# Four token tiles abreast in the first head, inverse rms by DRAM rows, and new shares in an encoder layer

## The chip, the cores and the metric

The kernel runs on one core of a Trainium2 chip. The metric is the device time of one execution in microseconds (us). TensorE (PE in the profile) multiplies, with the load of its stationary operand shown as PEld; VectorE (DVE), ScalarE (ACT) and GpSimd (POOL) do the elementwise work, and one queue, that of SyncE (SP), issues every DMA.

## The reference

One layer of a bidirectional encoder is applied to two requests of 1024 tokens and 1024 channels, in float32. Each request goes through the same steps:

```python
h = rms_norm(x, norm_g) * (1.0 + scale) + shift          # shift, scale, gate from silu(c) @ w_ada
qa, ka, va, za, qb, kb, vb, zb, ga, gb = split(h @ w_in)  # 5376 columns
oa = gqa_attention(rope(rms(qa)), rope(rms(ka)), va) * silu(za)     # 8 heads of 64, 2 kv heads
ob = rms_norm(diff_attention(rope(rms(qb)), rope(rms(kb)), vb, lam)) * silu(zb)  # 4 heads, 2 maps each
merged = sigmoid(ga) * (oa @ w_proj_a) + sigmoid(gb) * (ob @ w_proj_b)
y = x + gate * (merged @ w_out)
```

## The kernel before

Every factor of a projection is split into a high part that the multiplier takes exactly and a low part, the rest; a product is the sum of three matmuls (high by high, high by low, low by high). `load_w` loads a block of 256 columns of a weight in four pieces (two chunks of 128 channels each) and `split_w` makes the high part on ACT (L195) and the low part on POOL or, for every other piece while `alone[0]` is set, on DVE (L197).

**Start.** `start` loads the modulation weights in eight tiles; `ada` multiplies each (L330), `ada_end` copies the accumulator of each pair (L348) and lays it out as columns (L342). The first half of the first request's tokens is normalised and modulated there, chunk by chunk of 128 channels (chunks 4 to 7 later than 0 to 3, as their modulation comes last). The second half follows in `start_late`: its sums of squares (L297), an inverse root on POOL (L307), four transposes that spread it over all partitions (L314), one copy of that (L316), eight scalings on DVE (L418), and then per chunk two ACT operations and the low part on DVE (L423).

**Head.** `head` makes the keys and values of branch A with `kva_gen`: eight token tiles of 128, one after another, each of 24 matmuls 128x256 (`proj_tt`, L574) into a PSUM bank `f`. Behind each tile stands a chain: `rms` (ACT copies and squares, DVE sums, POOL takes the root, L597), the rope (L600 to L626), and, two tiles later, a transpose (L637) with the copies of `pairs_T`. With `alone[0]` set the rope is DVE's. Woven in are the gate products `z_gen` (24 matmuls 128x512, L764) and then the first queries.

**Order.** `weave` draws from several generators by shares and leads (the tables at the top of the file): attention steps, projections, gate pieces. From the order so recorded a scheduler makes each engine's own order, with priorities and with pairs that `behind` ties. In attention, scores go into one of two PSUM banks `s` (L798, L799), DVE takes the maximum and ACT the exponential (L802), DVE flips the probabilities (L843), DMAs place them as tile `q`, and PE multiplies them by the values (L866 and L883).

**End of a request.** `gated_gen` multiplies the attention outputs by their inverse sums. For branch A these go through DRAM: one transpose, a row, a store to `rA`, and broadcast loads. For branch B (`e` of 4 to 7) four transposes per half head (L970) spread the inverse rms into a PSUM bank, from which DVE scales (L971). `merge_gen` then projects branch A in 16 pieces of 12 matmuls and branch B in 16 more (L1038); the last `TAIL` pieces of branch A come after attention has ended.

## Time and profile before

| | |
|---|---|
| runs of the kernel | 1879.2, 1880.7 and 1883.36 us, median 1880.7 |
| span of the profiled execution | 1880.0 us |
| busy PE, DVE, ACT, POOL | 1836.5, 1222.3, 780.1, 607.1 us |
| mean granted clock of PE | 0.995 |
| DMA | 295.46 MB, mean 157 GB/s |

The span runs from the first to the last instruction of one profiled execution; the runs are of other executions. A busy PE is not PE at its peak, as matmuls are pipelined and their ends are modelled; so the distance from one start to the next is used below as the time of a matmul, not its mean duration.

### The profile page before, as it was taken

The numbers are of one execution on the slowest core, as the hardware profiler recorded it, in microseconds if no ns is written. First come the engines' busy times: TensorE is split into PE (matmuls) and PEld (weight loads), VectorE is DVE, ScalarE is ACT, GpSimd is POOL, SyncE is SP. The second block draws the span as 40 slices with busy tenths as digits, with TensorE's granted clock in tenths as the row PEclk, the third lists the DMA queues.
The fourth block names the chain that finished last, engine by engine and source line by source line (L and its number), as shares of the span: only waits on it lengthen the run. The fifth ranks groups of instructions, "written<-read, shape, count | busy, mean of one in ns | idle before, by whom it ended". The sixth has DMA issues, their size and how long they took to land.

```text
span 1880.0 us, 29891 instructions
## 1 busy us (share of the span) xinstructions
PE 1836.5 (98%) x10398; PEld 1550.6 (82%) x10398; DVE 1222.3 (65%) x2016; ACT 780.1 (41%) x1544; POOL 607.1 (32%) x888
## 2 busy tenths in 40 slices
PE   6999999999999999999999999999999999999999
PEld 3798877888899977888889888888888898888887
DVE  5777766454777777347466687666357766663795
ACT  4544434344554444313223445344345545442241
POOL 1243311433454451221233333014354635222100
PEclk8999999999999999999999999999999999999999
DMA  9135776555444567754631567666524343675442
GB/s 324 57 94 160 208 198 178 146 168 163 111 127 113 162 188 219 244 152 140 206 131 52 156 177 204 189 186 188 158 68 141 106 129 103 176 247 173 128 127 92
DMA packets 283895, 295.46 MB, mean 157 GB/s; under 512 B 41952, under 2 KB 236640, under 8 KB 283744
## 3 DMA queue, kind: packets, MB, share of 16 engines
q1 hardware_dynamic: 283744, 293.54, 53.1%
q8 instruction: 83, 1.36, 0.3%
q14 instruction: 68, 0.56, 0.1%
HBM read 133.98 MB, written 42.01 MB: 94 GB/s over the span
## 4 chain that ended last, share of the span: by engine, by line
PE 68%; DMA 4%; issue 3%; DVE 3%; SPq 3%; POOL 2%; ACT 1%; ACTq 0%; DVEq 0%; POOLq 0%
PE f L764 15%; PE f L574 15%; PE f L1038 7%; PE a L883 5%; PE s L798 4%; PE s L799 4%; PE a L866 4%; PE s L1038 3%; PE f L1073 3%; PE s L1073 2%; PE f L1145 2%; SPq L852 1%; DMA q<-p 1%; DMA st<-in_w_in_dram 1%; PE s L1145 1%
## 5 line engine op out<-in xcount | busy, mean ns | idle before, releaser
L764 PE MATMUL f<-u,w 128*128 128x512 f32 x2232 | 565.1, 395 | 0.8 <-POOL w L197 0.4
L574 PE MATMUL f<-w,u 128*128 128x256 f32 x3456 | 478.6, 287 | 0.9 <-POOL w L197 0.4
L764 PEld LDWEIGHTS f<-u,w 128*128 128x128 f32 x2232 | 409.8, 188 | 82.6 <-POOL w L197 1.1
L574 PEld LDWEIGHTS f<-w,u 128*128 128x128 f32 x3456 | 452.3, 193 | 22.3 <-issue 3.5
L800 DVE TENSOR_REDUCE m<-s 128x1 f32<-128x1024 f32 x256 | 309.6, 1218 | 98.8 <-PE s L799 97.4
L197 POOL TENSOR_TENSOR w<-st,w 128x512 fp32r<-128x512 f32 x160 | 213.2, 1350 | 357.9 <-ACT w L195 342.1
L843 DVE STREAM_TRANSPOSE p<-p 128x1024 f32<-128x1024 f32 x192 | 237.7, 1243 | 87.9 <-ACT p L802 73.5
L802 ACT ACTIVATE p<-s,m,u 128x1024 f32<-128x1024 f32 x128 | 153.9, 1204 | 160.0 <-issue 57.8
L802 ACT ACTIVATE p<-s,m,rsB 128x1024 f32<-128x1024 f32 x128 | 154.0, 1204 | 118.7 <-DVE m L801 97.1
L799 PE MATMUL s<-u,sw 128*128 128x512 f32 x512 | 201.1, 397 | 0.0
L195 ACT ACTIVATE w<-st 128x512 fp32r<-128x512 f32 x184 | 108.2, 626 | 112.4 <-DMA st<-in_w_in_dram 97.5
L1038 PE MATMUL f<-u,w 128*128 128x512 f32 x552 | 131.0, 392 | 0.0
L883 PE MATMUL a<-q,u 128*128 128x256 f32 x512 | 126.5, 380 | 4.0 <-DMA q<-p 3.7
L597 POOL TENSOR_TENSOR rsB<-ss,nhalf 128x4 f32<-128x4 f32 x64 | 68.1, 1064 | 184.7 <-DVE ss L596 160.6
L866 PE MATMUL a<-q,u 128*64 128x256 f32 x1024 | 117.7, 382 | 3.6 <-DMA q<-p 2.9
L1038 PEld LDWEIGHTS f<-u,w 128*128 128x128 f32 x552 | 103.0, 188 | 21.1
L798 PE MATMUL s<-u 128*128 128x512 f32 x256 | 107.9, 425 | 2.7 <-ACT p L802 2.7
L799 PEld LDWEIGHTS s<-u,sw 128*128 128x128 f32 x512 | 96.5, 189 | 16.4
L640 DVE TENSOR_TENSOR u<-f,u 64x256 fp32r<-64x256 f32 (+1 forms) x198 | 81.3, 411 | 42.9 <-ACT u L639 37.5
L883 PEld LDWEIGHTS a<-q,u 128*128 128x128 f32 x512 | 93.5, 190 | 18.8 <-issue 3.4
L772 ACT ACTIVATE ev<-f 128x512 f32<-128x512 f32 x93 | 55.3, 595 | 128.5 <-PE f L764 72.5
L866 PEld LDWEIGHTS a<-q,u 128*64 128x64 f32 x1024 | 73.8, 137 | 40.3 <-issue 7.2
(221 smaller groups left out, 2174.6 us busy)
## 6 DMA issues: line engine op xcount, KB each, us to landing
q<-p SPq DMA_DIRECT2D x768, 128.0 KB, 2.6
st<-in_w_in_dram SPq DMA_DIRECT2D x132, 256.0 KB, 3.3
zd<-ev SPq DMA_DIRECT2D x96, 256.0 KB, 2.7
sw<-u SPq DMA_DIRECT2D x256, 64.0 KB, 2.0
u<-in_w_ada_dram SPq DMA_DIRECT2D x8, 1024.0 KB, 11.7
oo<-zd SPq DMA_DIRECT2D x64, 128.0 KB, 2.4
od<-oo SPq DMA_DIRECT2D x64, 128.0 KB, 2.4
st<-in_w_in_dram SPq DMA_DIRECT2D x64, 128.0 KB, 2.7
```

Source lines behind the costliest of these rows:

```text
L195: hi = nc.scalar.activation(wh, st, AF.Copy)
L197: lo = e.tensor_tensor(out=wl, in0=st, in1=wh.bitcast(F32), op=ALU.subtract)
L574: ins = nc.tensor.matmul(ps, lt[c][:, sl], w[:, c, wi, :], start=(k == 0), stop=(k == 23))
L764: ins = nc.tensor.matmul(ps, w[:, c, wi, e * P : (e + 1) * P], rt[c], start=(k == 0), stop=(k == 23),)
L798: nc.tensor.matmul(s[:, sl], q, k[:, sl], start=True, stop=False)
L799: nc.tensor.matmul(s[:, sl], sw, k[:, sl], start=False, stop=True)
L800: nc.vector.tensor_reduce(out=m, in_=s, axis=AX.X, op=ALU.max, negate=True)
L802: nc.scalar.activation(pt.rearrange("p (j c a) -> p j c a", j=4, c=8), s.rearrange("p (c a j) -> p j c a", c=8, j=4), AF.Exp, bias=m, scal ...
L843: nc.vector.transpose(pt, pt)
L866: lambda k=k, m=m: nc.tensor.matmul(acc[(LO, HI)[m]], u["v"][:, k], pT[m][:, k], start=(k == 0), stop=(k == 7))
L883: nc.tensor.matmul(acc, u["v"][:, k], pT[:, k], start=(k == 0), stop=(k == 7))
L1038: nc.tensor.matmul(ps, w[:, c, wi, d * P : (d + 1) * P], o[:, oi, :], start=(k == 0), stop=(k == 11))
```

## The change

The first head of the first request is written anew. `abreast` puts four token tiles through each chunk of channels before the next chunk (two of their banks are halves of one `s` bank), twice for eight tiles; `kva_first` sets the fronts and transposes around it. The rope of tiles 1, 2, 3, 5 and 7 (`TURNS`) goes to POOL there, and so do two of eight low parts in `start_late`, whose spread now has room of its own in a `p` tile. `LATE` gives the second half's inverse root and scalings a priority. The first five gate blocks (`Z_HEAD`), not three, belong to that head. The last accumulator copy is tied ahead of DVE's weight splits, nine matmuls of the identity (`keep_busy`) follow the last two of the modulation weights, and branch B's small tables are tied behind the head's ropes on DVE.

For branch B the inverse rms of a head is transposed once, copied as a row, stored to a DRAM tile `rB` and loaded as a broadcast into a `tab` tile. All shares and leads of the weave get new values.

```diff
-Z_SHARE = (
-    (5, 16, 3, 1, 0, 17),
-    (6, 14, 2, 0, 3, 18),
-)
-Z_HEAD = (3, 3)
-Z_HEAD_A = (-0.35, -0.25)
-ATT_W = (
-    (1.0, 0.9, 1.1, 0.95, 1.0, 1.52),
-    (1.229, 1.265, 0.9, 1.0, 0.85, 1.069),
-)
-IN_A = (
-    (0.1, 0.05, 0.4, 0.05, -0.05, 0.1),
-    (0.1, 0.05, 0.4, 0.1, 0.15, 0.55),
-)
-Z_A = (
-    (0.15, 0.0, 0.2, -0.1, 0.0, 0.0),
-    (0.2, 0.05, 0.35, 0.05, 0.0, -0.1),
-)
-LAST_ATT, LAST_FILL = (48, 40)
+Z_SHARE = ((4, 15, 3, 1, 0, 20), (6, 14, 2, 0, 3, 18))
+Z_HEAD = (5, 3)
+LATE = (200, 3, 200)
+Z_AT = (2, 3)
+TURNS = (1, 2, 3, 5, 7)
+Z_HEAD_A = (-0.15, -0.05)
+ATT_W = ((1.1, 0.85, 1.1, 0.95, 1.05, 1.62), (1.229, 1.265, 0.8, 1.0, 0.85, 1.569))
+IN_A = ((-0.25, 0.25, 0.4, -0.05, -0.05, 0.15), (0.25, 0.0, 0.55, 0.1, 0.25, 0.7))
+Z_A = ((-0.25, 0.0, 0.2, -0.1, 0.05, 0.0), (0.2, 0.0, 0.35, 0.65, -0.3, -0.05))
+LAST_ATT, LAST_FILL = (47, 37)
 GATED_A = -0.2
-TAIL = 6
-TAIL_A = 0.3
+TAIL = 10
+TAIL_A = 0.05
 LAG = 2
...
-BEHIND = 1.4
-PAIRS = (1.05, 0.3)
+BUSY = (0, 0, 0, 0, 0, 0, 6, 3)
+BEHIND = 1.3
+PAIRS = (1.25, 1.4)
...
             prev = ins
+        return prev
...
-    def split_w(w, q, st):
+    def split_w(w, q, st, after=None):
         wh = w[:, q * 2 : q * 2 + 2, 0, :]
...
         lo = e.tensor_tensor(out=wl, in0=st, in1=wh.bitcast(F32), op=ALU.subtract)
+        if after is not None and e is nc.vector:
+            behind(lo, after)
         if ends and not alone[0]:
...
         for q, st in enumerate(sts):
-            split_w(w, q, st)
+            split_w(w, q, st, copied[0])
+    copied = [None]
...
-    def spread(rs):
+    def spread(rs, room=None):
...
             nc.tensor.transpose(bank[:, k * P : (k + 1) * P], rs[:, k : k + 1].to_broadcast([P, P]), ident)
-        rsb = mtile("ev", [P, 512], bufs=1)
+        rsb = mtile("ev", [P, 512], bufs=1) if room is None else room
         nc.scalar.activation(rsb, bank, AF.Copy)
...
     accs = {}
+    spare = ps_a.tile([P, 512], F32, tag="a", name=nm("a"))
+    def keep_busy(n, other):
+        for _ in range(n):
+            ins = nc.tensor.matmul(spare[:, :P], ident, ident, start=True, stop=True)
+            behind(ins, other)
+            other = ins
...
             accs[n // 2] = gbank()
-        across(accs[n // 2], q, [wt[:, c] for c in range(4)])
+        return across(accs[n // 2], q, [wt[:, c] for c in range(4)])
...
-        together([
+        return together([
             lambda c=c: nc.tensor.matmul(
...
         row = halves2(ptile())[0]
-        nc.vector.tensor_copy(row, acc)
+        copied[0] = nc.vector.tensor_copy(row, acc)
         ps = gbank()[:, :8].rearrange("p (c g) -> p c g", g=2)
...
         for n in range(8):
-            ada(n, wts[n])
+            last = ada(n, wts[n])
+            keep_busy(BUSY[n], last)
             if n == 3:
...
         sq = squares(xT[1])
-        return lambda: start_late(ht, xT, inv_rms(added(sq, end), latest[0]))
+        late_x.extend(xT[1])
+        return lambda: inv_rms(added(sq, end))
-    def start_late(ht, xT, rs):
-        rsb = spread(rs)
+    late_x = []
+    def start_late(ht, rs):
+        rsb = spread(rs, halves2(ptile())[0])
         for c in range(NCH):
-            x = xT[1][c]
+            x = late_x[c]
             if c % 4 == 0:
...
             nc.scalar.activation(ht[1][0][c], x, AF.Copy)
-            nc.vector.tensor_tensor(out=ht[1][1][c], in0=x, in1=ht[1][0][c].bitcast(F32), op=ALU.subtract)
+            e = nc.gpsimd if c % 3 == 2 else nc.vector
+            e.tensor_tensor(out=ht[1][1][c], in0=x, in1=ht[1][0][c].bitcast(F32), op=ALU.subtract)
...
             dma(gB[:, i, :], t[src][0].partition_broadcast(P))
-        nc.vector.tensor_scalar(out=gB[:, 0, :], in0=gB[:, 0, :], scalar1=SC, scalar2=None, op0=ALU.mult)
+        first = nc.vector.tensor_scalar(out=gB[:, 0, :], in0=gB[:, 0, :], scalar1=SC, scalar2=None, op0=ALU.mult)
+        behind(first, chained[1])
         nc.vector.tensor_tensor(out=gB[:, 1, 16:], in0=gB[:, 1, 16:], in1=gB[:, 0, 16:], op=ALU.mult)
...
         lamp = lamw[:, 4 * HD : 6 * HD].rearrange("p (a d) -> p a d", a=2)
-        nc.vector.tensor_tensor(
+        first = nc.vector.tensor_tensor(
             out=lamp, in0=lamv[:, 0::2, :], in1=lamv[:, 1::2, :], op=ALU.mult
         )
+        behind(first, chained[1])
         nc.vector.tensor_reduce(out=lam2, in_=lamp, axis=AX.X, op=ALU.add)
...
         dma(subg, t["subln_g"].rearrange("o e -> e o"))
-        nc.vector.tensor_scalar(out=subg, in0=subg, scalar1=0.5 * (1.0 - LAM_INIT) * math.sqrt(2 * HD), scalar2=None, op0=ALU.mult)
+        first = nc.vector.tensor_scalar(out=subg, in0=subg, scalar1=0.5 * (1.0 - LAM_INIT) * math.sqrt(2 * HD), scalar2=None, op0=ALU.mult)
+        behind(first, chained[1])
...
-    def kva_gen(ht, out):
+    lone = [False]
+    def kva_parts(ht, out):
         w = kva_w.pop()[0] if kva_w else load_w(w_cols(w_in, (C_KA, 256)))
...
         def front(tt, ps):
-            e = by_turns(tt)
+            e = nc.gpsimd if lone[0] and tt in TURNS else by_turns(tt)
             x3, s3 = rms(ps[:, :128], 2, e)
...
+        return w, front, back
+    def kva_gen(ht, out):
+        w, front, back = kva_parts(ht, out)
         yield from pipelined(ht, w, front, back, (0, 0))
+    def abreast(ht, w, hf):
+        both = sbank()
+        banks = [fbank()[:, :256], fbank()[:, :256], both[:, :256], both[:, 512:768]]
+        hh, hl = ht[hf]
+        for c in range(NCH):
+            for i, ps in enumerate(banks):
+                sl = slice(i * P, (i + 1) * P)
+                for n, (lt, wi) in enumerate(((hh, 0), (hh, 1), (hl, 0))):
+                    ins = nc.tensor.matmul(
+                        ps, lt[c][:, sl], w[:, c, wi, :], start=(c == n == 0), stop=(c == 7 and n == 2)
+                    )
+                    if latest[0] is None:
+                        behind(ins, picked[0])
+                    latest[0] = ins
+        return banks
+    def kva_first(ht, out, zs, late):
+        w, front, back = kva_parts(ht, out)
+        lone[0] = True
+        banks = abreast(ht, w, 0)
+        with tc.high_priority(offset=LATE[0]):
+            rs = late()
+        rows = [front(i, banks[i]) for i in range(3)]
+        drain(islice(zs, LATE[1]))
+        with tc.high_priority(offset=LATE[2]):
+            start_late(ht, rs)
+        drain(islice(zs, 6 - LATE[1]))
+        banks = banks + abreast(ht, w, 1)
+        for i in range(8):
+            back(i, rows[i])
+            if i < 5:
+                rows.append(front(i + 3, banks[i + 3]))
+            if i in Z_AT:
+                drain(islice(zs, 3))
+        lone[0] = False
     def qa_gen(st, half):
...
             dma(st["rA"], row)
+        if i > 1 and hf == 0:
+            for h in range(2 * i - 4, 2 * i - 2):
+                ps = fbank()[:NTT, :P]
+                nc.tensor.transpose(ps, st["ssB"][:, h], ident)
+                row = rtile()[:NTT, :P]
+                nc.scalar.activation(row, ps, AF.Copy)
+                dma(st["rB"][h * NTT : (h + 1) * NTT], row)
         rA = st["rA"].rearrange("(j h n) p -> j h (n p)", j=8, h=2)
+        rB = st["rB"].rearrange("(e h n) p -> e h (n p)", e=4, h=2)
         u = utile().rearrange("p (c s n) -> p c s n", c=2, s=2)
...
             dma(o, st["od"][e][hf])
+            rb = mtile("tab", [P, 512])
             if e < 4:
-                rb = mtile("tab", [P, 512])
                 for a in range(2):
...
             else:
-                rb = gbank()
-                for k in range(4):
-                    r = st["ssB"][:, e - 4, hf * 4 + k : hf * 4 + k + 1]
-                    nc.tensor.transpose(rb[:, k * P : (k + 1) * P], r.to_broadcast([P, P]), ident)
+                dma(rb, rB[e - 4, hf].partition_broadcast(P))
             nc.vector.scalar_tensor_tensor(out=o, in0=rb, scalar=subg if e > 3 else 1.0, in1=o, op0=ALU.mult, op1=ALU.mult)
...
         if g == 0:
-            for i in range(2):
-                drain(islice(kva, 6))
-                drain(islice(zs, 3))
-                if i == 0:
-                    late()
-            weave((chain(kva, qa), 40, 0.0), (islice(zs, nz - 6), nz - 6, Z_HEAD_A[g]))
+            kva_first(st["ht"], st, zs, late)
+            weave((qa, 26, 0.0), (islice(zs, nz - 12), nz - 12, Z_HEAD_A[g]))
         else:
...
         st["rA"] = dpool.tile([64, P], F32, name=nm("rA"))
+        st["rB"] = dpool.tile([4 * NTT, P], F32, name=nm("rB"))
         st["od"] = [
```

In each program's own order, DVE works as follows around the last accumulator copy (`p` from `f`) and the two splits of the first weight block (`w`). Before:

```order
L370 TENSOR_TENSOR u_277<-u_166,u_276 128x512 x3
L354 TENSOR_TENSOR modc<-f_301,bcol 128x8
L370 TENSOR_TENSOR u_277<-u_166,u_276 128x512
L197 TENSOR_TENSOR w_184<-p_185,w_184 128x2x256
L348 COPY p_311<-f_294 128x512
L197 TENSOR_TENSOR w_184<-p_188,w_184 128x2x256
L354 TENSOR_TENSOR modc<-s_313,bcol 128x8
L358 TENSOR_TENSOR modc<-modc,gcol 128x8
```

And with the change:

```order
L376 TENSOR_TENSOR u_280<-u_169,u_279 128x512 x4
L360 TENSOR_TENSOR modc<-f_310,bcol 128x8
L354 COPY p_323<-f_297 128x512
L191 TENSOR_TENSOR w_187<-p_188,w_187 128x2x256
L191 TENSOR_TENSOR w_187<-p_191,w_187 128x2x256
L360 TENSOR_TENSOR modc<-s_325,bcol 128x8
L364 TENSOR_TENSOR modc<-modc,gcol 128x8
L372 TENSOR_SCALAR u_170<-u_170,modc 128x512 x2
```

The copy has moved ahead of both splits. PE's order behind it: the layout of that copy (`pick`), and then the first key and value products, two matmuls by the high part of the input and one by its low part per chunk. Before:

```order
L342 MATMUL s_313<-pick,p_311 128x2 x4
L574 MATMUL f_361<-w_184,u_276 128x256 x2
L574 MATMUL f_361<-w_184,u_277 128x256
L574 MATMUL f_361<-w_184,u_276 128x256 x2
L574 MATMUL f_361<-w_184,u_277 128x256
L574 MATMUL f_361<-w_184,u_276 128x256 x2
L574 MATMUL f_361<-w_184,u_277 128x256
L574 MATMUL f_361<-w_184,u_276 128x256 x2
L574 MATMUL f_361<-w_184,u_277 128x256
```

And with the change:

```order
L336 MATMUL f_297<-u_185,cT 32x512 x4
L323 MATMUL a_111<-ident 128x128 x3
L348 MATMUL s_325<-pick,p_323 128x2 x4
L729 MATMUL f_374<-w_187,u_279 128x256 x2
L729 MATMUL f_374<-w_187,u_280 128x256
L729 MATMUL f_375<-w_187,u_279 128x256 x2
L729 MATMUL f_375<-w_187,u_280 128x256
L729 MATMUL s_373<-w_187,u_279 128x256 x2
L729 MATMUL s_373<-w_187,u_280 128x256
L729 MATMUL s_373<-w_187,u_279 128x256 x2
L729 MATMUL s_373<-w_187,u_280 128x256
```

One tile (bank `f_361`) took four chunks in a row; now four tiles (`f_374`, `f_375` and the two halves of `s_373`) take each chunk in turn, and dummies (`a` from the identity) stand ahead of the layout. The other place is PE at the end of the first request's attention, where branch A's projection (`f` or `s` from `u` and `w`) begins. Before:

```order
L970 MATMUL s_8341<-ident,ssB_120 128x128 x4
L1038 MATMUL f_8151<-u_7372,w_8131 128x512 x6
L1038 MATMUL f_8151<-u_7683,w_8131 128x512 x6
L970 MATMUL f_8167<-ident,ssB_120 128x128 x4
L1038 MATMUL f_8177<-u_7372,w_8131 128x512 x6
L1038 MATMUL f_8177<-u_7683,w_8131 128x512 x6
```

And with the change:

```order
L1100 MATMUL f_8250<-u_7512,w_8149 128x512 x6
L1100 MATMUL f_8250<-u_7790,w_8149 128x512 x6
L1015 MATMUL f_8264<-ident,ssB_121 8x128
L1100 MATMUL s_8284<-u_7790,w_8149 128x512 x4
L1100 MATMUL s_8350<-u_7340,w_8314 128x512 x6
L1015 MATMUL f_8269<-ident,ssB_121 8x128
L1100 MATMUL s_8350<-u_7645,w_8314 128x512 x6
```

The groups of four transposes, of which three more follow the rows shown, have become single ones of eight rows; behind the second of those shown come 108 matmuls of branch A's projection, and then the first product of branch B that uses heads 2 and 3.

## The prediction

> **What bounds the kernel now.** I read the page's busy times first, then the busy times in stretches, then the instructions in order of time where a stretch shows idle TensorE, and the waits last. The page:
>
> ```profile
> span 1880.0 us, 29891 instructions
> ## 1 busy us (share of the span) xinstructions
> PE 1836.5 (98%) x10398; PEld 1550.6 (82%) x10398; DVE 1222.3 (65%) x2016; ACT 780.1 (41%) x1544; POOL 607.1 (32%) x888
> ```
>
> TensorE (PE) sets the end; no other engine is near. So an edit pays only if it takes matmuls away, takes away idle PE, or raises PE's clock. Where idle PE lies, by stretch (columns: stretch, its length, busy time of PE, PEld, DVE, ACT, POOL, granted clock, DMA share, GB/s):
>
> ```profile
> 0.00:39.40 39.40, 21.87 (x109) 10.48 (x109) 20.40 (x35) 13.93 (x24) 8.62 (x12) 0.89 0.99 363
> 39.40:85.70 46.30, 41.72 (x259) 37.29 (x259) 37.26 (x107) 26.89 (x67) 9.33 (x11) 0.91 0.20 60
> 85.70:700.00 614.30, 608.52 (x3736) 518.76 (x3735) 415.71 (x674) 280.41 (x565) 242.41 (x384) 1.00 0.55 154
> 700.00:1000.00 300.00, 296.73 (x1428) 249.17 (x1427) 170.37 (x275) 94.43 (x186) 70.26 (x62) 1.00 0.55 176
> 1000.00:1640.00 640.00, 632.18 (x3816) 540.30 (x3815) 421.69 (x690) 293.24 (x580) 242.02 (x390) 1.00 0.53 147
> 1640.00:1880.00 240.00, 235.51 (x1061) 194.56 (x1059) 156.86 (x236) 71.24 (x124) 34.41 (x31) 1.00 0.49 153
> ```
>
> Half of the 43.5 us of idle PE is in the first 85.7 us, and the clock is below one only there. The first 39.4 us run at a DMA share of 0.99: the loading of the modulation weights, which the change leaves. The second stretch, the first head's projections, is what it rebuilds.
>
> **The first head.** PE in order of time:
>
> ```profile
> 37.68 1.84 PE L342 MATMUL s<-pick,p 128*128 128x2 f32 x8 [3.44 <-DVE p L348]
> 39.38 8.05 PE L574 MATMUL f<-w,u 128*128 128x256 f32 x48
> ...
> 57.25 0.30 PE L637 MATMUL s<-ident,row 128*128 128x128 f32 x1 [1.56 <-DVE row L626]
> 58.02 1.11 PE L314 MATMUL f<-ident,rs 128*128 128x128 f32 x4 [0.47 <-POOL rs L307]
> ...
> 65.75 5.63 PE L764 MATMUL f<-u,w 128*128 128x512 f32 x24
> 71.22 2.20 PE L574 MATMUL f<-w,u 128*128 128x256 f32 x17
> ...
> 82.67 0.30 PE L637 MATMUL f<-ident,row 128*128 128x128 f32 x1 [1.05 <-DVE row L626]
> 82.73 3.12 PE L574 MATMUL f<-w,u 128*128 128x256 f32 x24
> 85.69 0.27 PE L637 MATMUL s<-ident,row 128*128 128x128 f32 x1
> ```
>
> By 85.69 PE has done the 192 products of keys and values and 48 of the gates (two row groups). A group of 24 of the first kind takes 85.69 - 82.73 = 2.96 us, one of the second 71.22 - 65.75 = 5.47 us. So 8 and 2 groups are 23.7 + 10.9 us, and the sums, spreads and transposes between add an estimated 2.4: 37.0 us of work in 46.3. The other 9.3 us are lost, to waits and to the clock (here with PE's columns only; the two halved stretches end at 44.1 and 61.1):
>
> ```profile
> 27.00:30.40 3.40, 0.90 (x8) 1.00 1.07 394
> 30.40:44.10 13.70, 10.15 (x46) 0.50 0.88 287
> 54.30:57.70 3.40, 1.69 (x8) 1.00 0.27 77
> 57.70:61.10 3.40, 3.08 (x15) 0.50 0.29 108
> 1000.00:1003.20 3.20, 1.31 (x10) 1.00 0.03 9
> 1003.20:1006.60 3.40, 3.40 (x19) 0.50 0.56 169
> ```
>
> Each time, a stretch of 3.4 us with PE busy half of it or less (0.90, 1.69, 1.31) is followed by half the clock. At half the clock an estimated half of the time is lost: (44.1 - 39.4)/2 = 2.4 and 3.4/2 = 1.7 us, 4.1 together; the idle times quoted are 3.1, smaller ones the rest.
>
> The change does four things here. **Start.** The last accumulator copy (L348) comes off DVE ahead of the two weight splits (L197). DVE and POOL then:
>
> ```profile
> 34.58 0.68 DVE L370 TENSOR_TENSOR u<-u,u 128x512 fp32r<-128x512 f32 x1
> 35.29 1.65 DVE L197 TENSOR_TENSOR w<-p,w 128x512 fp32r<-128x512 f32 x1
> 36.85 0.68 DVE L348 COPY p<-f 128x512 f32<-128x512 f32 x1
> 37.45 1.16 DVE L197 TENSOR_TENSOR w<-p,w 128x512 fp32r<-128x512 f32 x1
> ...
> 60.45 5.39 DVE L418 SCALAR_TENSOR_TENSOR u<-u,modc,ev 128x512 f32<-128x512 f32 x8 [2.75 <-ACT ev L316]
> ```
>
> ```profile
> 34.81 3.25 POOL L197 TENSOR_TENSOR w<-p,w 128x512 fp32r<-128x512 f32 x2 [7.39 <-ACT w L195]
> ```
>
> The copy can start at about 35.4 and not 36.85, so PE's first projection starts 1.45 us earlier, at 37.9. The splits, now behind it, end near 38.6; the second weight piece is wanted only after 24 of the abreast products (3 us), so the move costs nothing there.
>
> **Order.** Before, two tiles run through chunks 0 to 3, wait for the second half of the normalised input, and finish; gate products and transposes follow, each behind a DVE chain of one tile. Now four tiles go through each chunk: 48 products before chunk 4 is wanted, 48 more after it. In the changed order the transposes of these eight tiles stand behind gate work or other tiles, at least 6.8 us of PE's own work (products counted at the two rates above) behind their projection; before, two stood 3 us behind, so the waits of 1.56 and 1.05 go, and with the first of them the second halving of the clock. What is late next is the second half of the tokens: PE reaches its tiles after 37.9 + 11.8 + 10.9 + 2, plus clock, about 65 us; their low parts come from DVE behind the eight scalings (L418), which ended at 65.84. Six of those eight low parts stay on DVE, two go to POOL. I expect PE to wait 1 to 2 us there. The bounds are 0 and 5: POOL now works the rope of tiles 1 and 2 meanwhile, and a two-input DVE operation beside a POOL one took 1.65 and 1.16 us where one alone took 0.68, so each of the eight may lose up to 0.5.
>
> **Clock.** Nine dummy matmuls (L323) follow the seventh and eighth weight tiles. They fill gaps and cost nothing: PE waits 3.44 us for the copy anyway. Their time is not in the trace; the nearest row is the transpose below, 0.09 us each, and the six make the stretch from 27.0 busy 0.90 + 0.54 to 1.1. As 1.69 was followed by the lower clock, I take it that it falls all the same and comes back one or two stretches of 3.4 us into dense work, at 40.7 or 44.1: 1.4 or 3.1 us, 2.3 taken. By the Trainium skill, "TensorE: Matmul & The Clock Gate", Part 1, the clock halves only after an idle window of 3.4 us; by that rule the dummies hold it and the 2.3 us go too. The rows here speak against it: after 54.3, half busy, the clock fell.
>
> Sum: 37.9 + 37.0 + 2.3 + 1.5 (wait) + 0.8 (small ones, as now) = 79.5, against 85.7: **6.2 us**, between 1.5 (wait 5, clock 3.1) and 10.
>
> **Head of the second request.** Its projections stall once:
>
> ```profile
> 1001.81 0.30 PE L637 MATMUL f<-ident,row 128*128 128x128 f32 x1 [1.45 <-DVE row L626]
> ```
>
> The transposes of the last tile but one stand there 24 products (3 us) behind that tile. In the changed order every tile of this head has at least 6 us between, because its first gate products are dealt among the tiles (Z_HEAD_A -0.05 for -0.25). At 6 us the first head's tiles did not wait. So 1.45 us go, and the halved clock after 1003.2, 3.4/2 = 1.7: **3.1 us**, bounds 0 and 3.1.
>
> **Inverse rms of branch B.** Before, 16 groups of four transposes spread it:
>
> ```profile
> 771.26 0.60 PE L970 MATMUL f<-ident,ssB 128*128 128x128 f32 x4
> 771.62 0.71 PE L764 MATMUL f<-u,w 128*128 128x512 f32 x2
> ```
>
> A group takes 771.62 - 771.26 = 0.36 us of PE, 5.8 in all; eight single transposes at 0.09 take their place, 0.7. That is **5.0 us** off PE, where PE is never idle. New are 8 row copies on ACT, 8 small stores and 16 broadcast loads on the one DMA queue (SP). The nearest row is branch A's same path:
>
> ```profile
> DMA to landing us min/median/max: 2.2/3.1/5.4
> ```
>
> A store, a load and the DVE and ACT steps behind them are 2 x 3.1 + 2 = 8 us, at worst 13. It is late only for heads 2 and 3, and there 108 products of branch A's projection (24.6 us at 5.47 per 24) stand between the last new transpose and the first product that needs it, since TAIL goes from 6 to 10 pieces. Queued behind a waiting broadcast on SP are gate loads for the same projection; PE has five PSUM banks there, 2.7 us each, before it feels one. So the cover holds; were it gone, up to 5 us would come back. DVE's scaling reads the row from SBUF and not PSUM: same size, not on the path.
>
> **Shares.** The weights of the weave move attention steps among projections and gates; the number of matmuls stays. What they can win or lose are the waits behind attention:
>
> ```profile
> PE s L798 <- ACT p L802: 4.2, 6, 1.2
> PE a L883 <- DMA q<-p: 3.7, 4, 1.5
> ```
>
> (engine, tile, line, releaser: us in total, times, longest). In the changed order 14 value products of 64 stand under 12 us of PE's work behind their last scores, 8 before; 7 scores of 252 under 4 us behind the pair whose bank they take, 1 before. By that it is a little tighter; transposes are looser. I take 0, bounds -7 and +7 (the two rows' sum, 7.9, could nearly go or double).
>
> **Sum.** 6.2 + 3.1 + 5.0 + 0 = 14.3 of the profiled 1880.0 us gives 1865.7. The median of the three runs, 1880.7 (1879.2 to 1883.4), lies 0.7 above this span, so 1866.
>
> **Rivals.**
> 1. POOL's new rope work delays the second half (wait 5 us and, with PE half idle for 3.4 us, another halving). The first head then gives 1 us: 1871. For it: 1.65 against 0.68 us. Against: POOL has only some 10 small operations there. By the Trainium skill, "SBUF — State Buffer", section "SBUF: two separate sides", a DVE operation with two SBUF inputs and a POOL one exclude each other for a whole instruction; the split rows agree.
> 2. The dummies hold the clock, as the page's rule has it: 2.3 us more, 1864.
> 3. The new shares cut attention's waits by 5 to 7 us: 1860.
> 4. The broadcast rows come late in both requests, or SP's queue holds up the tail: 5 us each time, 1876.
> 5. Slower: values placed nearer to their scores make PE wait for the flipped probabilities (q<-p). Today 4 of the waits for L883 cost 0.9 us each. It decides against the change from some 20 more such waits, 18 us, over 14.3 + 3.8: 1885. Of 64 units six more are tight, so it is unlikely.
>
> **How the numbers follow.** A measurement of this kernel tells 0.2%, 3.8 us, from no change: 1876.9 is the edge of faster, 1884.5 that of slower. Chances: the sum above 0.50, rival 1 0.15, rival 2 0.12, rival 3 0.10, rival 4 0.08, rival 5 0.05. The sum and rivals 1 to 3 are faster, 0.87; rival 4 sits at the edge and gives 0.02 to faster and 0.06 to no change; with 0.05 slower that leaves 0.89, 0.06 and 0.05. The range, 1858 to 1876, takes in rivals 1 to 3 and the bounds of the shares, and leaves out rival 5 and half of rival 4.
>
> **What would show it.** Abreast products starting near 38 us, with no row of idle PE over 1 us until about 63; PE done with the first head's 192 + 48 products near 79.5. Granted clock: 1.0 from 44 us on and at 1003 right; another dip near 65 is rival 1, 1.0 from 30 on is rival 2. No PE row of four ssB transposes, PE busy down by some 5 us, no wait for a tile computed from the broadcast row. The sum of PE's idle between 85.7 and 1000 and between 1000 and 1640 (9.1 and 7.8 now) within 7 us of this. The prediction is wrong if the idle behind attention grows by more than 10, or if the first head ends after 84.

## The result, and the profile after

The changed kernel takes 1872.5 us (median of four runs, 1868.3 to 1873.2) where the kernel before takes 1881.3: a ratio of 0.9948, 95% interval 0.9935 to 0.9962. A second comparison, on another occasion, gave 1875.2 to 1883.8 us, 0.9960 (0.9947 to 0.9972). So the change is worth some 8 to 9 us. The prediction was 1866, in a range of 1858 to 1876, and its sum was 14.3 us: direction and range held, and the gain was overrated by more than half.

The profiled execution of the change is the shortest of its four: 1866.5 us of span, where the others had 1870.2 to 1871.4. So I read a second profiled execution of the same program beside it (span 1872.5). The page of the first:

```profile
span 1866.5 us, 29868 instructions
## 1 busy us (share of the span) xinstructions
PE 1828.7 (98%) x10360; PEld 1546.5 (83%) x10360; DVE 1213.4 (65%) x1984; ACT 781.5 (42%) x1552; POOL 628.5 (34%) x920
```

PE in order of time, in the first head (start, length, engine, line, operation, tiles, count, and in brackets the idle time before the row and what ended it):

```profile
36.06 1.02 PE L348 MATMUL s<-pick,p 128*128 128x2 f32 x8 [2.59 <-DVE p L354]
36.94 1.07 PE L729 MATMUL f<-w,u 128*128 128x256 f32 x6
...
62.85 0.40 PE L729 MATMUL s<-w,u 128*128 128x256 f32 x2
66.23 0.51 PE L729 MATMUL f<-w,u 128*128 128x256 f32 x2 [2.98 <-DVE u L434]
...
77.24 0.27 PE L651 MATMUL s<-ident,row 128*128 128x128 f32 x1
77.27 5.70 PE L821 MATMUL f<-u,w 128*128 128x512 f32 x24
...
85.21 0.30 PE L651 MATMUL f<-ident,row 128*128 128x128 f32 x1 [2.02 <-ACT u L705]
86.39 8.45 PE L821 MATMUL s<-u,w 128*128 128x512 f32 x24 [0.88 <-ACT u L705]
```

Three things are to be seen. The products abreast (L729) start at 36.94, a microsecond sooner than predicted. From there to 77 PE is idle ahead of one row only, the 2.98 us in front of the second half. And the 192 + 48 products are done at 77.3 (85.69 before), but then come two waits and 24 products that take 8.45 us instead of 5.70. The clock tells why (stretch, length, busy PE and its products, granted clock, DMA share, GB/s):

```profile
34.23:37.64 3.41, 1.58 (x14) 1.00 1.04 352
37.64:41.05 3.41, 3.41 (x19) 0.50 0.98 263
...
80.00:85.42 5.42, 3.40 (x17) 1.00 0.49 148
85.42:92.25 6.83, 5.95 (x15) 0.50 0.22 76
...
110.00:980.00 870.00, 863.54 (x4875) 1.00 0.57 168
980.00:1050.00 70.00, 69.94 (x475) 1.00 0.27 82
1050.00:1700.00 650.00, 644.84 (x3762) 1.00 0.57 160
```

The same long stretches of the kernel before:

```profile
110.00:980.00 870.00, 860.95 (x4838) 1.00 0.57 167
980.00:1050.00 70.00, 68.11 (x451) 0.98 0.19 58
1050.00:1700.00 650.00, 643.33 (x3775) 1.00 0.57 161
```

And the second execution of the change, where the clock was halved from 36.31 to 43.13, from 67.03 to 73.85, from 90.92 to 94.33 and from 101.16 to 104.57:

```profile
36.31:43.13 6.82, 6.82 (x34) 0.50 0.87 225
43.13:80.00 36.87, 33.91 (x217) 0.91 0.18 55
80.00:110.00 30.00, 25.31 (x127) 0.89 0.29 88
```

To set programs of different order against each other I worked out the time that PE has lost by a point: the start of the product that runs there, less the pitch at full clock of every product before it (0.2275 us for 128x512, 0.1195 for a projection's 128x256, 0.09 for a transpose, and so on, the same for all; dummies left out). It holds waits and halved clock together (differences below are taken of unrounded values):

```
lost by (us)        60     80    110    980   1050   1700   PE's own work   span
before            36.4   38.3   40.1   69.4   74.0   97.5       1777.8     1880.0
change            28.2   31.6   38.7   65.1   66.2   89.2       1772.8     1866.5
change, again     29.7   35.7   44.3   70.1   71.3   95.9       1772.8     1872.5
```

Of the two differences, 13.5 and 7.5 us, 5.0 is work of PE (its own work), 3.5 the second request's head (4.6 lost between 980 and 1050 before, 1.1 now). In the attention of the first request 26.4 and 25.9 us are lost instead of 29.3, in that of the second 23.1 and 24.6 instead of 23.5. And the first head? At 80 us the change is 6.7 and 2.6 us ahead; at 110 it is 1.4 ahead in one execution and 4.2 behind in the other. **The gain of the first head is made by 77 us and given back by 110.** The row of the kernel before is one execution; its medians in the comparisons below lie between 1880.4 and 1884.5 us, so a few us of such a difference can be that execution's own.

### The profile page after: what moved, and what is told of

Its sections match the earlier page's. It is cut to its first block, busy times and chain, and to the rows that moved or that the text cites. A ratio compares the mean times of both kernels' runs of the same rounds, so it can differ in the third digit from the quotient of the medians.

```text
span 1866.5 us, 29868 instructions
## 1 busy us (share of the span) xinstructions
PE 1828.7 (98%) x10360; PEld 1546.5 (83%) x10360; DVE 1213.4 (65%) x1984; ACT 781.5 (42%) x1552; POOL 628.5 (34%) x920
## 5 line engine op out<-in xcount | busy, mean ns | idle before, releaser
L821 PE MATMUL f<-u,w 128*128 128x512 f32 x2160 | 544.7, 395 | 0.0
L821 PEld LDWEIGHTS f<-u,w 128*128 128x128 f32 x2160 | 397.8, 188 | 80.6 <-issue 1.2
L588 PE MATMUL f<-w,u 128*128 128x256 f32 x3264 | 440.6, 284 | 0.1
L588 PEld LDWEIGHTS f<-w,u 128*128 128x128 f32 x3264 | 421.3, 191 | 17.2 <-issue 1.5
L1100 PE MATMUL f<-u,w 128*128 128x512 f32 x516 | 120.6, 389 | 0.0
L1100 PEld LDWEIGHTS f<-u,w 128*128 128x128 f32 x516 | 96.9, 188 | 20.1
L653 ACT ACTIVATE u<-f 64x256 fp32r<-64x256 f32 (+1 forms) x200 | 73.0, 365 | 85.1 <-DVE u L654 56.4
```

Source lines behind the costliest of these rows:

```text
L588: ins = nc.tensor.matmul(ps, lt[c][:, sl], w[:, c, wi, :], start=(k == 0), stop=(k == 23))
L821: ins = nc.tensor.matmul(ps, w[:, c, wi, e * P : (e + 1) * P], rt[c], start=(k == 0), stop=(k == 23),)
L1100: nc.tensor.matmul(ps, w[:, c, wi, d * P : (d + 1) * P], o[:, oi, :], start=(k == 0), stop=(k == 11))
```

## The experiments

**The change once more, and the change without one part.** In the first group one part at a time is undone: the dummies, the rows, and the order of the first head. The change itself ran again in the second group. The main lines of each edit are shown; `...` marks lines left out.

```diff
@@ without dummies @@
-BUSY = (0, 0, 0, 0, 0, 0, 6, 3)
+BUSY = (0, 0, 0, 0, 0, 0, 0, 0)
@@ old rows @@
...
-                dma(rb, rB[e - 4, hf].partition_broadcast(P))
+                rb = gbank()
+                for k in range(4):
+                    r = st["ssB"][:, e - 4, hf * 4 + k : hf * 4 + k + 1]
+                    nc.tensor.transpose(rb[:, k * P : (k + 1) * P], r.to_broadcast([P, P]), ident)
...
@@ old head @@
-        return lambda: inv_rms(added(sq, end))
+        return lambda: inv_rms(added(sq, end), latest[0])
...
-            kva_first(st["ht"], st, zs, late)
-            weave((qa, 26, 0.0), (islice(zs, nz - 12), nz - 12, Z_HEAD_A[g]))
+            for i in range(2):
+                drain(islice(kva, 6))
+                drain(islice(zs, 3))
+                if i == 0:
+                    start_late(st["ht"], late())
+            weave((chain(kva, qa), 40, 0.0), (islice(zs, nz - 6), nz - 6, Z_HEAD_A[g]))
```

> The changed kernel itself, once more, on the chip on which the others of this group run, so that each of them can be set against it and not only against the kernel before. If its first comparison (0.9948) holds on any chip, its ratio is 0.9935 to 0.9962 and it beats the runs of the first group that lack one part (0.9962 without the dummies, 0.9979 with the old transposes, 0.9971 with the old head). The rival: the part of the gain that lay in one lucky profiled execution (1866.5 us of span where three others took 1870.2 to 1871.4) is not there again, the ratio is 0.9960 to 0.9975, and then the dummies and the abreast head are worth less than 2 us each and the row of transposes carries most of the gain. In either case the profile should show again the wait of about 3 us near 63 us behind the subtractions of the second half, and the wait of 2 us or more near 83 us with a halved clock behind it.

> The changed kernel without the nine dummy matmuls. The prediction's step: the clock falls at the same place with or without them, so no more than 1 us either way. The rival, that they hold the clock: it falls at 30.4 us as in the kernel before and comes back at 40.7 or 44.1 instead of falling at 37.6 for one stretch, so the layout and the first 20 to 30 of the abreast products run at half the clock: 2 to 3.5 us slower than the changed kernel, about 1874.5 to 1876 against its 1872.5.

> The changed kernel with branch B's inverse rms spread by 64 transposes into PSUM again. The prediction: PE takes 5.0 us more, all of it on the path: about 1877.5 against 1872.5. The rival, that the transposes ran beside something PE waited for anyway: under 2 us. The second request's attention order moves a little with it, so the stretches at the ends of the two requests are read beside the total.

> The changed kernel with the first head's keys and values tile after tile again (ropes on DVE, transposes two tiles later), the copy ahead of the splits, the dummies, the shares and the rows kept. The prediction gave the head 6.2 us, of which 1.45 is the copy: undoing the order costs 4 to 5 us. The reading of the changed trace: the order won 8 us by 80 us and lost 5 again by 95 us to the wait for ACT at 82.9 and the halved clock behind it; undoing it costs 0 to 3 us.

Measured: the change again 1875.2 us, 0.9960 (0.9947 to 0.9972); without dummies 1876.6, 0.9962 (0.9950 to 0.9974); with the old transposes 1880.2, 0.9979 (0.9967 to 0.9991); with the old order of the head 1877.7, 0.9971 (0.9961 to 0.9982). The rival of the first text comes nearest: the rows carry the largest part of the gain (4.9 us between the medians, 3.6 and 5.8 by the change's two ratios), the order of the head is worth 2 to 4 us by these ratios and not 6, the dummies 0.4 to 2.6, which is not told from nothing. (Without the dummies a block of 14 gate products near 97 us changed its place too.) With the old rows the 64 transposes are back, 56 of them in banks `f`; with the old order one wait ended the head, and it lost 47.9 us by 110 (the products that read `ssB`, then PE in order of time):

```profile
L1027 PE MATMUL f<-ident,ssB x56: 270/273/303, 766.4 to 1749.7; 128*128 128x128 f32 x56
```

```profile
96.92 0.45 PE L651 MATMUL f<-ident,row 128*128 128x128 f32 x1 [7.41 <-DVE row L640]
```

The kernel before has no such wait in its first head (3.44 us is its longest), so this mixture prices the old order too badly rather than too well, and still it costs only 2 to 4 us.

**What ends the waits near 83 us.** ACT and DVE of the change, there:

```profile
82.92 0.63 ACT L189 ACTIVATE w<-st 128x512 fp32r<-128x512 f32 x1 [2.30 <-DMA st<-in_w_in_dram]
83.57 0.60 ACT L829 ACTIVATE ev<-f 128x512 f32<-128x512 f32 x1
84.06 0.27 ACT L605 ACTIVATE row<-f 128x128 f32<-128x128 f32 x1
```

```profile
83.58 0.69 DVE L191 TENSOR_TENSOR w<-st,w 128x512 fp32r<-128x512 f32 x1 [0.96 <-ACT w L189]
84.19 0.28 DVE L634 TENSOR_TENSOR rc<-row,tab 128x128 f32<-128x128 f32 x1
```

The fourth weight rounding of the next projection waits for its transfer, and behind it stand the copies of tiles 5 to 7 (L605, L705) on ACT and the rotation of tile 4 (L634) on DVE. Two kernels move it: all four roundings behind tile 5's copy, then only the fourth behind tile 7's.

(`copies` holds the copies of L705 by tile; the first line of each stands at the end of `kva_first`, the others in `split_w`.)

```diff
@@ four roundings @@
+        held.extend([copies[5]] * 4)
+        if held:
+            behind(hi, held.pop())
@@ the fourth alone @@
+        held[:] = [copies[7]]
+        if held and q == 3:
+            behind(hi, held.pop())
```

> The changed kernel with the four ACT operations of the weight block loaded behind the first head tied behind the front of the sixth tile; PE's order is the same, matmul for matmul. Theory one: the wait at 82.9 us is ACT's queue, where a weight piece that waits for its DMA stands ahead of the fronts of the last tiles; then the 2.9 us of waits go and with them the halved clock from 85.4 to 92.3: 4 to 6 us faster than the changed kernel, 1866.5 to 1868.5. Theory two: the fronts wait for their three row buffers, that is for PE's own transposes, whatever ACT does: PE still waits 1.5 us or more, the clock still halves, at most 2 us faster.

> The change with one instruction of ACT moved: the fourth rounding of the weights for the first projection behind the head (which in the change's profile waited 2.30 us for its transfer until 82.92 us, ahead of the copies of tiles 5 to 7) is tied behind the last of these copies; its remainder on DVE goes with it. Run with all four roundings tied behind tile 5's copy, the first wait there fell from 2.02 to 0.81 us but 1.68 us of roundings then stood ahead of tile 6 and 7 and POOL's remainders (2.95 us) ahead of the norms, and waits of 2.52 and 2.51 us took its place. If the one instruction is the cause, DVE's rotation of tile 4 is done near 83.3 and not 85.1 us, the wait of 2.02 us falls to about 1.0, the block of products behind it starts at 85.3 instead of 86.4 us, and the kernel gains 1.1 us, or up to 3.9 if the clock is not halved behind the shorter wait (the 24 products took 8.45 us there, 5.70 at full clock). The rival: the copies of tiles 5 to 7 wait in any case for the eviction and for the third row buffer, the wait stays within 0.5 us of 2.9 in sum, and the time is the change's.

Measured: 1878.6 us, 0.9969 (0.9958 to 0.9979), and 1875.7 us, 0.9963 (0.9950 to 0.9976). Neither gains. PE with all four moved, then with one:

```profile
84.77 0.33 PE L654 MATMUL f<-ident,row 128*128 128x128 f32 x1 [0.81 <-ACT u L709]
87.62 7.29 PE L826 MATMUL s<-u,w 128*128 128x512 f32 x24 [2.52 <-ACT u L709]
...
98.10 0.47 PE L654 MATMUL f<-ident,row 128*128 128x128 f32 x1 [2.51 <-POOL row L643]
```

```profile
85.53 0.33 PE L654 MATMUL f<-ident,row 128*128 128x128 f32 x1 [0.81 <-ACT u L709]
86.85 7.38 PE L826 MATMUL s<-u,w 128*128 128x512 f32 x24 [0.98 <-ACT u L709]
...
95.73 0.70 PE L826 MATMUL s<-u,w 128*128 128x512 f32 x2 [1.28 <-DVE ev L836]
97.15 0.33 PE L654 MATMUL f<-ident,row 128*128 128x128 f32 x1 [0.72 <-POOL row L643]
```

The wait of 2.02 falls to 0.81 in both (the second text had said about 1.0; the first, either that all of it goes or that 1.5 us or more stay), and the time does not follow. With all four moved 2.52 and 2.51 us take its place, with one 0.98, 1.28 and 0.72, and the clock is halved there all the same (7.29 and 7.38 for 24 products). The 2.52 us end with the copy of a last tile's values (L709, L705 in the change) out of its bank `s`, which the gate products need next: the four tiles hold their PSUM banks until ACT comes to them. By the table's measure the change lost 7.1 and 8.6 us between 80 and 110, the two kernels 10.0 and 6.6. So the rounding set where the wait fell, not that there was one. The theory of the one instruction fell.

**What ends the wait near 63 us.** Two causes were open: POOL's norms and rotations slow DVE's scalings (rival 1), or the remainders stand behind all eight scalings in DVE's queue.

The rows of DVE in the change, in order of time:

```profile
58.19 7.18 DVE L428 SCALAR_TENSOR_TENSOR u<-u,modc,p 128x512 f32<-128x512 f32 x8
...
65.50 1.54 DVE L434 TENSOR_TENSOR u<-u,u 128x512 fp32r<-128x512 f32 x2
```

One run gives POOL's norms and rotations to DVE, one sets the order on DVE (in `start_late`), one does both.

```diff
@@ ropes on DVE @@
-TURNS = (1, 2, 3, 5, 7)
+TURNS = ()
@@ remainders in turn @@
+        subs = []
-            nc.vector.scalar_tensor_tensor(
+            add = nc.vector.scalar_tensor_tensor(
+            if c >= 4 and (c - 4) % 3 != 2:
+                behind(add, subs[c - 4])
-            e.tensor_tensor(out=ht[1][1][c], in0=x, in1=ht[1][0][c].bitcast(F32), op=ALU.subtract)
+            subs.append(e.tensor_tensor(out=ht[1][1][c], in0=x, in1=ht[1][0][c].bitcast(F32), op=ALU.subtract))
```

> The change with the norms and rotations of the first head's five tiles that it deals to POOL given back to DVE (an empty list of turns). In the change the eight operations of line 428 on DVE took 7.18 us while POOL worked on those tiles, against 5.39 us in the kernel before, and PE then waited 2.98 us near 63 us for the second half. If POOL's operations slow DVE's, line 428 falls back to 5.4 us here. What that is worth: by one theory the wait near 63 us shrinks by 1.8 us and the kernel gains 1 to 2 us; by the rival, DVE, which then runs two tiles' norms (some 2 us of small operations at 0.29 us each) ahead of the second half, is as late as before, the wait stays at 3 us or grows, and the chain of tiles 3, 5 and 7 on DVE adds to the wait near 83 us: no gain, or 1 to 3 us of loss.

> The change with one order laid down on DVE: in the second half of the first head, the scaling of chunk c (line 428) waits for the remainder of chunk c-4 (line 434) where DVE does both, so that the first remainder is not queued behind all eight scalings. In the change's profile the eight scalings ran from 58.19 to 65.37 us and the first remainder at 65.50, so PE waited 2.98 us (2.96 to 3.0 in its repeats) for it near 63 us; the cast that the first remainder needs was done at 61.2 us. If the wait is the queue on DVE, the first remainder is done near 62 us, the wait falls to under 0.5 us and the kernel gains 2 to 3 us on the change (a ratio of 0.9945 to 0.995 where the change has 0.9960 and 0.9948). If what limits is the casts on ACT (1.33 us a chunk from 59.1 us on, against 1.44 us of products), small waits of some tenths of a us come at each chunk instead, 1 to 2 us in sum, and the gain is 1 to 2. If the lost time is given back near 83 us, as the earlier start makes PE reach tiles 5 to 7 sooner, the time does not change.

> The order of the run before this one (scalings and remainders in turn on DVE) and, beside it, the norms and rotations of the first head's five tiles on DVE instead of POOL, as in the run that took 0.9946 of the kernel before. If POOL's contention and DVE's queue are two causes, both gains add up: the scalings at 0.67 us each, the wait near 63 us under 0.5 us, and a ratio of 0.993 to 0.994. If they are one (the wait near 63 us), it is no faster than either alone. The rival: DVE, which now does everything, falls behind between 62 and 72 us, the remainders of chunks 4 to 7 are late and PE stops there: slower than either by 1 to 3 us.

Measured: 1871.8 us, 0.9946 (0.9928 to 0.9963); **1868.3 us, 0.9917 (0.9903 to 0.9932)**; 1869.1 us, 0.9924 (0.9910 to 0.9939). The scalings on DVE between 55 and 75 us (busy time in all, mean ns of one, idle before), of the change and of the first of the three:

```profile
L428 DVE SCALAR_TENSOR_TENSOR u<-u,modc,p 128x512 f32<-128x512 f32 x8 | 7.2, 965 | 0.0
```

```profile
L428 DVE SCALAR_TENSOR_TENSOR u<-u,modc,p 128x512 f32<-128x512 f32 x8 | 5.4, 754 | 0.0
```

The contention is real: with POOL's norms and rotations gone the scalings take 754 ns instead of 965, as in the kernel before (748). By the Trainium skill, "SBUF — State Buffer", section "SBUF: two separate sides", a DVE operation with two SBUF inputs and a POOL one that reads SBUF exclude each other. These rows agree in that DVE is slower beside POOL; the exclusion itself they do not show. But it is not what most of the wait hangs on: the wait only falls from 2.98 to 2.08, and the time is 0.4 and 2.6 us below the change's by the two ratios, which is not told from nothing. With the remainders in turn and POOL's work left where the change has it:

```profile
58.16 4.04 DVE L429 SCALAR_TENSOR_TENSOR u<-u,modc,p 128x512 f32<-128x512 f32 x5
...
62.46 0.81 DVE L437 TENSOR_TENSOR u<-u,u 128x512 fp32r<-128x512 f32 x1
63.19 0.94 DVE L429 SCALAR_TENSOR_TENSOR u<-u,modc,p 128x512 f32<-128x512 f32 x1
64.06 0.95 DVE L437 TENSOR_TENSOR u<-u,u 128x512 fp32r<-128x512 f32 x1
```

```profile
67.07 0.50 PE L732 MATMUL f<-w,u 128*128 128x256 f32 x2 [0.32 <-POOL u L437]
...
88.33 0.30 PE L654 MATMUL s<-ident,row 128*128 128x128 f32 x1 [1.03 <-DVE ev L834]
...
96.94 0.33 PE L654 MATMUL f<-ident,row 128*128 128x128 f32 x1 [2.15 <-POOL row L643]
```

The first remainder comes at 62.46 instead of 65.50, at the slow rate of 0.8 to 0.95 us an operation, and 0.32 us are left of the wait. It is better than expected: 0.0031 and 0.0043 below the two ratios of the change, 6 to 8 us, of which the wait is 2.7; the medians are 4 and 7 us apart. The scheduler's order changed with the edit too: a third block of 24 gate products now stands ahead of the last transpose, where the change has two. And the clock stayed full from 40.2 to 98.3 us: from 60 to 110 it was halved for 3.4 us, in the change's two profiles for 6.8 and 13.7. Lost by 80: 29.6 us (31.6 and 35.7 in the change), by 110: 36.0 (38.7 and 44.3); so most of the lead is there by 80, before that block, as a shorter wait and, against the second profile, as a clock that is not halved at 67. Both edits together are no faster than this one, as the case of one wait in their text has it. How much of the gain in time the wait is worth, and how much the scheduler's order, was not taken apart.

**The clock at the start.** Does more dummy work hold it, and is it worth that?

The second kernel here has the remainders in turn as well.

```diff
@@ 14 dummies @@
-BUSY = (0, 0, 0, 0, 0, 0, 6, 3)
+BUSY = (0, 0, 0, 0, 0, 0, 6, 14)
@@ 12 dummies, remainders in turn @@
-BUSY = (0, 0, 0, 0, 0, 0, 6, 3)
+BUSY = (0, 0, 0, 0, 0, 0, 6, 12)
```

> The change with 14 dummy products instead of 3 behind the last matrix-vector products of the head, 22 passes more of 0.09 us, or 2.0 us, in the wait of 2.59 us that PE had before 36.06 us. In the profiles so far the clock was halved in that stretch in all but one (from 36.31 to 43.13, 37.64 to 41.05, 37.04 to 40.45 us: 1.7 to 3.4 us lost each). If PE's work in the stretch before decides, the clock is 1.0 at the start of the products abreast and the gain is 1.5 to 3 us. If the dummies run at the halved clock already, they take 5 us and delay the start by 1 to 2.5 us. If the stretch in which the clock is halved is only moved behind, into the first 10 us of the products or to the waits near 63 and 83 us, the time does not change.

> The order that took 0.9917 of the kernel before (scalings and remainders of the second half in turn on DVE) and 12 dummy products instead of 3 behind the last matrix-vector products (18 passes more of 0.09 us, 1.6 us, in PE's wait of 2.59 us before 36 us). With 14 dummies and the change's own order on DVE the clock was 1.0 at the start of the products abreast, but PE's order between 78 and 101 us had shifted too, PE lost 10.5 us there where the change lost 7.2, and the time was 5 us longer than the change's. Here PE's order behind 78 us is that of the run of 0.9917. If a held clock at the start is worth what it saves there (a stretch of 3.4 us at half clock, 1.7 us), the ratio is 0.990 to 0.991. If the loss with 14 dummies was theirs and not the order's (each stretch in which the clock is halved comes anyway, only later), the ratio is 0.9917 or more, with halved stretches between 60 and 105 us that the run of 0.9917 did not have.

Measured: 1880.5 us, 0.9977 (0.9965 to 0.9989), and 1869.3 us, 0.9943 (0.9926 to 0.9961). The stretch before the products abreast with 14 dummies, and one far behind it:

```profile
33.05:36.46 3.41, 3.41 (x32) 1.00 1.05 401
36.46:43.29 6.83, 6.83 (x60) 1.00 0.82 214
...
695.22:698.63 3.41, 1.40 (x11) 1.00 0.39 108
698.63:708.87 10.24, 10.24 (x31) 0.50 0.63 174
```

The dummies fill the wait and the clock holds: the products start at full clock. (They also did in two profiles with the change's own nine dummies, those with the four roundings moved and with both edits on DVE, where the wait was 0.2 us.) The time is not better. In the first kernel halved stretches came between 67 and 105 us, and one of 10.24 us in the attention, behind this wait:

```profile
697.90 0.50 PE L855 MATMUL s<-u 128*128 128x512 f32 x1 [2.01 <-ACT p L859]
```

In the change's second profile that wait is 1.02 us and the clock stays full. The 5 us between the two medians are about what this one stretch costs (10.24/2), but it was seen in one execution; that the dummies brought it on is not shown, since PE's order between 60 and 101 us had shifted with them too. In the second kernel, with that order left alone, the median is that of the remainders in turn alone, 1868.3, within 1 us, and its ratio is higher; what a held clock at the start saves (1.7 us, half of the 3.4 that the profile of the remainders in turn has at half clock there) does not show. Part of it is seen to go: PE came to the second half 1.6 us sooner and waited 1.33 us for it, not 0.32.

**The old shares under the new head.**

The change's head, dummies and rows, with `Z_SHARE`, `Z_HEAD_A`, `ATT_W`, `IN_A`, `Z_A`, `LAST_ATT`, `LAST_FILL`, `TAIL`, `TAIL_A`, `BEHIND` and `PAIRS` of the kernel before; `Z_HEAD` stays (5, 3).

```diff
-Z_SHARE = ((4, 15, 3, 1, 0, 20), (6, 14, 2, 0, 3, 18))
+Z_SHARE = (
+    (5, 16, 3, 1, 0, 17),
+    (6, 14, 2, 0, 3, 18),
+)
...
-TAIL = 10
+TAIL = 6
...
-BEHIND = 1.3
-PAIRS = (1.25, 1.4)
+BEHIND = 1.4
+PAIRS = (1.05, 0.3)
```

> The change with the kernel before's tables of shares (how projections, gate pieces and attention are dealt), but with its abreast head, its dummies and its rows through DRAM. The prediction priced the shares at 0, with 7 us either way, apart from the stop at the second request's start (1.45 us of wait and a halved clock, 3.1 us in all), which it put down to the new tables. By the prediction this is slower than the change by 3.1 us, with that stop and a halved clock near 1000 us back in the profile, and the waits of attention between 110 and 1000 us and between 1050 and 1640 us within 3 us of the change's in sum. By the rival (the third of the prediction: shares that cut the waits of attention by 5 to 7 us) it is slower by 8 to 10 us. If the old tables lose nothing, the stop at 1000 us belongs to how the first request ends and not to the tables.

Measured: 1901.1 us, 1.009 (1.0068 to 1.0111), 26 us slower than the change. PE's waits between 110 and 1050 us, and its stretches (columns as above):

```profile
PE f L663 <- DVE row L652: 4.8, 1, 4.8
PE a L952 <- DMA q<-p: 3.9, 3, 2.6
```

```profile
110.00:980.00 870.00, 852.82 (x4728) 0.99 0.56 165
980.00:1050.00 70.00, 65.17 (x442) 0.98 0.24 74
```

None of the three forecasts holds. PE is idle 17 us between 110 and 980 (6.5 in the change), and 20.5 us at half clock come on top. The stop at the second head is back, and longer (4.8). So the tables do not carry over from one head to another: between 110 and 980 the old ones lose 29.3 us under the old head and 49.8 under the new. This does not mean that the new tables won 26 us for the change: it loses 26.4 us there, against 29.3 in the kernel before. One misfit is plain in the edit: of 48 gate blocks the head and the first five phases take 3 + 25 in the kernel before and 5 + 23 in the change, which leaves 20 for the last phase; here they take 5 + 25 and leave 18. Which of the tables it is, was not taken apart.

## Why the prediction was right and wrong

**Rows: right.** 5.0 us were predicted. That PE's own work falls by 5.0 is the same count of products at the same 0.09 us; the test that does not rest on it is the run with the old transposes, 4.9 us slower by the medians. The cover holds: DVE waits for the broadcast, PE does not (the change's waits between 780 and 850 us, and the transfers' median time to landing):

```profile
DVE row L1033 <- DMA tab<-rB: 11.3, 5, 4.4
```

```profile
tab<-rB SPq DMA_DIRECT2D x16, 256.0 KB, 4.4
```

The landing took 4.4 us where branch A's path gave 3.1. In the second request DVE waits longer for these rows (16.5 us at most) and PE still does not. Rival 4 did not come.

**Head of the second request: right.** 3.1 predicted, 3.5 measured in both profiles; no wait and a full clock at 1003. With the old tables the stop came back, with the old order of the first head it did not.

**Shares: right within their bounds.** 0 was taken; 2.9 and 3.4 us came in the first request's attention, 0.4 and -1.1 in the second's, 2.8 in the mean of the two profiles, within the bounds of 7. Rivals 3 and 5 did not come.

**First head: the step that failed.** The 6.2 us were summed up to the last of the 192 + 48 products, at 79.5. That point came at 77.3, and at 81.4 in the second execution, but the agreement is luck in part, as errors cancelled. The start was 1.0 and 0.5 us early. The work, with the small waits, took about 35.2 us and not 37.0 + 0.8. The wait for the second half was 3.0 us, not 1.5: the sum had it behind the eight scalings on DVE, as it was, but PE came to it at 63.25 and not at 65, and each scaling took 0.2 us more beside POOL. The clock came back, on average, about where I put it; the second halving, at 67.03 in the second execution (3.1 us), stood in rival 1 only.

What was wrong is the sentence that the transposes stand at least 6.8 us behind their projection, with the conclusion that the waits go. That distance was counted in PE's work. For tiles 4 to 7 the chain begins with the copies on ACT, and these do not start when PE ends: an eviction, a weight rounding, and the row buffers that the first tiles still hold stand ahead. In the place of the two waits that went came waits of 2.02, 0.88 and 0.69 us between 85 and 96 and 6.83 us at half the clock; the sign "1.0 from 44 us on" failed. The landmark hid this: at 77.3 the transposes of two of the eight tiles are done, in the kernel before, at 85.69, those of five. I should have gone on counting to the first projection behind the head, where both orders have done the same; there the term is 1.4 and -4.2 us instead of 6.2, and by the run with the old order 2 to 4. By the profiles it falls short by 4.8 and 10.4, and the attention's 2.8 give part of that back. That other engines' queues cause it is shown where an experiment moved the wait (DVE near 63 us); for the 80 to 110 us it is read from the releasers, and no run has emptied that stretch, so the cause there stays open: between 60 and 110 us the kernel before loses 3.7 us, the change 10.5 and 14.6, the remainders in turn still 7.8.

By its time the result lies nearest to rival 1 (1871), and one of the change's two executions has the halved clock near 67 us that it names. But its mechanism, POOL's contention, adds 0.2 us to each scaling and is the smaller part: taken away it leaves 2.08 of the 2.98 us, and with it in place the wait all but goes once DVE's order is changed.

**Clock.** I took the dummies for too little to hold it, and that was half right. In the change's first profile the clock is full at 30.4, where the kernel before had lost it, and falls at 37.64, behind the wait of 2.59 us that the dummies did not fill. Without them it fell at 33.35 for 10.24 us; but with them it fell at 31.26 under the old shares and at 31.86 with the rotations on DVE, so that they held it is not shown. The six and three dummies took 1.60 and 0.94 us; the 0.54 to 1.1 us reckoned for the six were too little. Rival 2 (1.0 from 30 on) did not come in the change's profiles, but the full clock at the start was seen with 14 dummies, and no gain in time with it.

**The median.** I set 0.7 us between span and median. The profiled executions of the change take 1.8 us more than their span, so a span of 1865.7 is a time of 1867.5; read so, the median was missed by 5.0 us and not by 6.5.

## What to carry to other kernels

A term that ends at a landmark has to go on until both versions have done the same work and the queues of the other engines are empty; a head that is faster by 8 us at one row can be level, or behind, 30 us later. When a consumer works through chunks, look whether its producer's queue holds all first steps ahead of the first last step: one ordering constraint on DVE (scaling of chunk c behind the remainder of chunk c-4) was, with the order that the scheduler made of it, worth nearly as much as the whole change: 0.9917 of the kernel before (0.9924 and 0.9943 in the two other kernels with it), against 0.9948 and 0.9960. And tables that deal filler work can be fitted to the stage before them: judge them together, or the part that is undone is charged with time that is not its own, here 26 us.

## What was not expected of the hardware

The halved stretches come in whole multiples of 3.41 us (3.41, 6.83, 10.24). In nine of the thirteen profiles of the change and its variants PE waited 1.0 to 3.5 us for the last copy near 36 us, and the clock was halved for some of the first 10 us behind; in the other four the wait was at most 0.6 us, and it was full. By the Trainium skill, "TensorE: Matmul & The Clock Gate", Part 1, a whole idle window of about 3.4 us is needed; here stretches busy 1.58 and 1.40 of 3.41 us were enough, so the measurement says less idle time does it. The same order of instructions, run twice, had 3.4 and 6.8 us of half clock at the start and none and 6.8 us at 67 us: when a wait falls into the window differs from one execution to the next, and the spread of 5 us between executions of the change is of that size; that it is the clock's alone is not shown. The halved stretch of 10.24 us behind a wait of 2.01 us, with 14 dummies, is the dearest in the attention: the same wait on ACT was one microsecond shorter in the change's second profile, where the clock stayed full, and the longer one was followed by a loss of five.
